# Low halves of the weights by an accumulating transfer: every fourth half unit of a split-fp32 decoder trunk

## The chip, the cores and the metric

The kernel runs on one core of a Trainium2 chip. The core has TensorE (in the profile PE for its matmuls and PEld for its weight loads), VectorE (DVE), ScalarE (ACT), GpSimd (POOL) and SyncE (SP, which here only issues transfers), 16 DMA engines, and its on-chip memories SBUF and PSUM. Each engine has a queue of its own and they wait for one another through semaphores. The metric is the time of one execution on the device in microseconds (us); lower is better.

## What is computed

The reference is a decoder trunk of two layers over 256 tokens of width 1024, in float32. Each layer is a half-step SwiGLU FFN, a mixer in which an SSD branch and a gated DeltaNet branch run side by side, and a second FFN:

```python
for l in range(DEPTH):
    h = h + 0.5 * swiglu(rms_norm(h, ffn1_norm[l]), ffn1_w_in[l], ffn1_w_out[l])
    u = rms_norm(h, mix_norm[l])
    (z_s, xbc, dt_s, qkv, z_d, b_d, a_d, gate_s, gate_d) = jnp.split(u @ w_in[l], split_points, axis=-1)
    y_s = mamba2_branch(...)
    y_d = deltanet_branch(...)
    merged = (jax.nn.sigmoid(gate_s) * (y_s @ ssm_w_branch[l])
              + jax.nn.sigmoid(gate_d) * (y_d @ dn_w_branch[l]))
    h = h + merged @ w_out[l]
    h = h + 0.5 * swiglu(rms_norm(h, ffn2_norm[l]), ffn2_w_in[l], ffn2_w_out[l])
return rms_norm(h, final_norm)
```

Nearly all of the work is matrix products with weights that are read once from HBM: 504 pieces of 128 x 1024 float32, 512 KB each.

## The kernel before

Precision comes from splitting. A float32 operand is written as a high part in the format float32r (fp32r in the profile) and a low part, the rest that the high part leaves; a product is then three matmuls: high by high, high by low, low by high. The activations are split when they are produced (uTh and uTl for the normed input, gh and gl inside the FFN, bh and bl in the branches, mh and ml for the merged output). The weights are split when they arrive.

The weights lie in the one array `wst`, in the order in which they are used. A *half unit* j is half of one of its rows, a tile of 128 x 1024. Three functions handle them:

- `load(j)` (line 93) issues the transfer of half j on SP into a buffer `wraw`, of which there are NRAW = 5.
- `prep(j)` (line 98) takes the raw tile, gets buffers `whi` and `wlo` (NSPL = 5 of each), lets ACT copy the raw tile into `whi` in float32r (line 102, shown as L60 in the profile because the helper `act` records it), and lets DVE subtract: `wlo` = `wraw` - `whi` (line 103, shown as L63, the helper `tt`).
- `take()` (line 111) hands the next half to the matmuls. It first issues the loads up to 9 halves ahead, and the preps up to 5 halves ahead. With five buffers the prep of half j can begin when the matmuls on half j-5 are done.

At the end of an FFN and of a mixer (`close`) the last five halves are taken together, and `state["hold"]` keeps further preps back until the norm that follows has its own instructions in the queues; `norm_in` then lets them go in small steps.

The users of the halves are: `tok_chunk` (four halves at a time, or two; tiles f and t), `chan_chunk` (two halves, 48 matmuls with 256 moving columns each; tiles fc in the FFN, kk, qq, vv, bc, zd, xs and g in the mixer), `branch` (two halves; b) and `out_chunks` (one, two or five halves; o). One FFN takes 66 halves: 4, then 40 in twenty chan chunks, then 22. A mixer takes 120. A layer is 252 halves, a multiple of four. In a chan chunk the order is: two passes, each over the eight row blocks, first the four of the first half, then the four of the second. The weights of the chan chunks and branches are the stationary operand; in the others they are the moving one.

The list ORDER sets by hand in which sequence the mixer's chunks and its small steps follow one another. The order of instructions on each engine is otherwise the scheduler's, by priority and by order in the program; the norms run with raised priority (`tc.high_priority(offset=PRI)`).

POOL has little to do: the inverse square roots as a power (`rsqrt`, line 118, in the profile L119; tiles zz, so, srr and c) and some memsets.

Of the kernel before, what the change touches and what calls it, by code (L numbers as in the profile page):

```python
# [11 lines left out]
ALU = mybir.AluOpType  # L12
# [33 lines left out]
def trunk_kernel(ctx, tc, x, wst, wsm, norms, lpar, rpar, cst, out):  # L46
    nc = tc.nc
    V, A, G, PE = nc.vector, nc.scalar, nc.gpsimd, nc.tensor
# [10 lines left out]
    def act(o, i, func=AF.Copy, **kw):  # L59
        return A.activation(out=o, in_=i, func=func, **kw)  # L60

    def tt(o, a, b, op):
        return V.tensor_tensor(out=o, in0=a, in1=b, op=op)  # L63
# [9 lines left out]
    def f(ap):  # L73
        return ap.bitcast(F32)
# [23 lines left out]
    def prep(j):  # L98
        r = raws.pop(j)
        hi = wpool.tile([P, 1024], F32R, tag="whi", name="whi", bufs=NSPL)  # L100
        lo = wpool.tile([P, 1024], F32R, tag="wlo", name="wlo", bufs=NSPL)
        act(hi[:], r[:])
        tt(lo[:], r[:], f(hi[:]), ALU.subtract)
        halves[j] = (hi, lo)

    def ahead(key, n, fn):
# [4 lines left out]
    def take():  # L111
        j = state["taken"]
        state["taken"] = j + 1
        ahead("loaded", j + NSPL + NRAW - 1, load)
        ahead("prepped", j + 1 if state["hold"] else j + NSPL, prep)
        return halves.pop(j)
# [46 lines left out]
    def rstd_of(t):  # L163

        ss = small([P, 2], "ss")
        for n in range(2):
            junk = tmp2("junk")
            act(junk[:], h[:, t, n * 512 : (n + 1) * 512], AF.Square, scale=1.0 / 32.0, accum_out=ss[:, n : n + 1])
        z = small([P, 2], "zz")
        ts(z[:, 0:1], ss[:, 0:1], ss[:, 1:2], ALU.add, EPS, ALU.add)  # L170
        rsqrt(z[:, 1:2], z[:, 0:1], [P, 1])
        return z[:, 1:2]
# [18 lines left out]
    def norm_in(nw, add=None):  # L191

        for t in range(2):
            with tc.high_priority(offset=PRI):
                if add:
                    add(t)
                ins, done = rms_chain(t, nw)
            if t == 0:
                state["hold"] = False
                n = state["taken"]  # L200
                if not add:
                    ahead("prepped", n + 1, prep)
                    with tc.issue_after(done[0].ins), tc.issue_after(done[1].ins):
                        ahead("prepped", n + START, prep)
                with tc.issue_after(ins.ins):
                    ahead("prepped", n + 2, prep)
# [819 lines left out]
    for t in range(2):  # L1026
# [5 lines left out]
        r = rstd_of(t)  # L1032
# [123 lines left out]
```

## Time and profile before

| | |
|---|---|
| time before, median of 2 runs | 1603.12 us (1601.9 to 1604.35) |
| span of the profiled execution, first to last instruction | 1602.4 us |
| granted TensorE clock, mean | 0.999 |
| HBM read | 280.94 MB |
| bytes moved by transfers | 284.86 MB, mean 178 GB/s |
| DMA engines, share of their time in packets (main queue) | 53.2% |

The page gives a span for the profiled execution and no other time of it; the span differs from the median of the runs by 0.7 us. The page lists the busy time of each engine, the same in 40 slices, the transfers' queues, the chain of work that ended last and the costliest groups of instructions, each as "line, engine, operation, output <- inputs, shape, count | busy us, mean ns of one | idle time of the engine just before them and what ended it". A timeline row is "start, duration, engine, line, operation, output <- inputs, shape, count [idle before <- what ended it]". A row of a tile's view gives "minimum/median/maximum duration in ns, first to last start in us".

### The profile page before, as it was taken

What the parts mean: (1) busy time and instruction counts of PE and PEld (TensorE: products, weight loads), DVE (VectorE), ACT (ScalarE), POOL (GpSimd) and SP (SyncE); (2) the same over time, 40 slices, a digit from 0 to 9 for tenths busy, and PEclk for the clock granted to TensorE, in tenths of its full rate; (3) what the DMA queues carried; (4) which work ended last, traced back from release to release, by engine and by line L of the source; (5) the groups of instructions that cost most, each with busy time, mean ns of one, the idle gap of its engine ahead of it and who ended that gap; (6) DMA issues with size and microseconds to landing.
All of it is one profiled execution on the core that took longest, in us unless ns stands there. A gap on an engine that the chain in (4) does not pass through costs nothing.

```text
span 1602.4 us, 30733 instructions
## 1 busy us (share of the span) xinstructions
PE 1582.4 (99%) x12624; PEld 1470.5 (92%) x12624; DVE 1068.2 (67%) x1546; ACT 882.5 (55%) x1418; POOL 59.1 (4%) x60
## 2 busy tenths in 40 slices
PE   8999999999999999999999999999999999999998
PEld 7999879999999998999899987899999999989986
DVE  5555468957899667555465555699579986665554
ACT  5444468756665545444354444686656664454443
POOL 0000020000000000000000001000000000000000
PEclk9999999999999999999999999999999999999999
DMA  7555465553455446555565555555335554555552
GB/s 263 191 187 195 162 203 189 165 156 117 170 199 177 143 161 201 191 187 197 171 205 190 185 197 179 188 182 186 115 130 201 170 172 159 180 174 188 191 199 94
DMA packets 91923, 284.86 MB, mean 178 GB/s; under 512 B 22069, under 2 KB 23045, under 8 KB 90758
## 3 DMA queue, kind: packets, MB, share of 16 engines
q1 hardware_dynamic: 91782, 282.90, 53.2%
q8 instruction: 99, 1.62, 0.4%
q14 instruction: 42, 0.34, 0.1%
HBM read 280.94 MB, written 1.92 MB: 177 GB/s over the span
## 4 chain that ended last, share of the span: by engine, by line
PE 91%; DVE 4%; DMA 2%; ACT 1%; POOL 1%; issue 1%; SPq 0%; POOLq 0%; DVEq 0%; ACTq 0%
PE fc L215 9%; PE fc L216 9%; PE fc L217 9%; PE o L211 5%; PE o L210 5%; PE o L209 5%; PE b L216 3%; PE b L217 3%; PE b L215 3%; PE t L209 2%; PE t L210 2%; PE xs L216 2%; PE xs L215 2%; PE t L211 2%; PE xs L217 2%; PE g L217 1%
## 5 line engine op out<-in xcount | busy, mean ns | idle before, releaser
L63 DVE TENSOR_TENSOR wlo<-wraw,whi 128x1024 fp32r<-128x1024 f32 x504 | 612.4, 1223 | 382.1 <-ACT whi L60 379.8
L60 ACT ACTIVATE whi<-wraw 128x1024 fp32r<-128x1024 f32 x504 | 529.2, 1059 | 436.9 <-PE fc L216 177.2
L215 PE MATMUL fc<-uTh,whi 128*128 128x256 f32 x1280 | 357.9, 280 | 0.0
L216 PE MATMUL fc<-uTl,whi 128*128 128x256 f32 x1280 | 357.3, 279 | 0.0
L217 PE MATMUL fc<-uTh,wlo 128*128 128x256 f32 x1280 | 356.7, 279 | 0.0
L216 PEld LDWEIGHTS fc<-uTl,whi 128*128 128x128 f32 x1280 | 240.7, 188 | 0.2
L215 PEld LDWEIGHTS fc<-uTh,whi 128*128 128x128 f32 x1280 | 240.6, 188 | 0.2
L217 PEld LDWEIGHTS fc<-uTh,wlo 128*128 128x128 f32 x1280 | 240.6, 188 | 0.0
L209 PE MATMUL o<-whi,gh 128*128 128x512 f32 x352 | 137.3, 390 | 0.0
L210 PE MATMUL o<-wlo,gh 128*128 128x512 f32 x352 | 137.2, 390 | 0.0
L211 PE MATMUL o<-whi,gl 128*128 128x512 f32 x352 | 137.0, 389 | 0.0
L215 PE MATMUL b<-bh,whi 128*128 128x256 f32 x384 | 108.9, 286 | 1.2 <-ACT bh L60 1.2
L216 PE MATMUL b<-bl,whi 128*128 128x256 f32 x384 | 108.5, 283 | 0.7 <-DVE bl L63 0.7
L217 PE MATMUL b<-bh,wlo 128*128 128x256 f32 x384 | 108.1, 283 | 0.0
L211 PEld LDWEIGHTS o<-whi,gl 128*128 128x128 f32 x352 | 66.1, 188 | 13.6
L209 PEld LDWEIGHTS o<-whi,gh 128*128 128x128 f32 x352 | 66.1, 188 | 13.5
L210 PEld LDWEIGHTS o<-wlo,gh 128*128 128x128 f32 x352 | 66.1, 188 | 13.5
L215 PEld LDWEIGHTS b<-bh,whi 128*128 128x128 f32 x384 | 73.2, 192 | 1.7 <-ACT bh L60 1.7
L216 PEld LDWEIGHTS b<-bl,whi 128*128 128x128 f32 x384 | 73.6, 192 | 1.1 <-DVE bl L63 1.1
L217 PEld LDWEIGHTS b<-bh,wlo 128*128 128x128 f32 x384 | 73.5, 192 | 0.0
L215 PE MATMUL xs<-uTh,whi 128*128 128x256 f32 x256 | 73.0, 285 | 0.0
L215 PE MATMUL g<-uTh,whi 128*128 128x256 f32 x256 | 72.6, 284 | 0.0
(265 smaller groups left out, 3250.6 us busy)
## 6 DMA issues: line engine op xcount, KB each, us to landing
wraw<-in_wst_dram SPq DMA_DIRECT2D x504, 512.0 KB, 4.0
dc<-rdram SPq DMA_DIRECT2D x8, 1024.0 KB, 7.0
nw<-in_norms_dram SPq DMA_DIRECT2D x6, 512.0 KB, 4.9
gb<-rdram SPq DMA_DIRECT2D x8, 256.0 KB, 5.9
h<-in_x_dram SPq DMA_DIRECT2D x4, 256.0 KB, 3.2
out_dram<-fo SPq DMA_DIRECT2D x4, 256.0 KB, 2.3
dq<-X SPq DMA_DIRECT2D x2, 256.0 KB, 4.3
cs<-in_cst_dram SPq DMA_DIRECT2D x1, 384.0 KB, 9.7
```

What stands on the lines that cost most here:

```text
L60: return A.activation(out=o, in_=i, func=func, **kw)
L63: return V.tensor_tensor(out=o, in0=a, in1=b, op=op)
L209: PE.matmul(ps, lh, rh, start=start, stop=False)
L210: PE.matmul(ps, lh, rl, start=False, stop=False)
L211: PE.matmul(ps, ll, rh, start=False, stop=stop)
L215: PE.matmul(ps, wh, mh, start=start, stop=False, skip_group_check=shared)
L216: PE.matmul(ps, wh, ml, start=False, stop=False, skip_group_check=shared)
L217: PE.matmul(ps, wl, mh, start=False, stop=stop, skip_group_check=shared)
```

## The change

In `prep`, every half unit with j % 4 == 3 gets its low part another way. ACT first writes the negated high part into `wlo` (a second activation with scale -1), and then a transfer issued from POOL reads the same half of the weights from HBM once more and adds it onto `wlo`: -high + weight. The other three quarters of the halves keep the subtraction on DVE. The raw tile of such a half is read by the first copy alone.

```diff
         hi = wpool.tile([P, 1024], F32R, tag="whi", name="whi", bufs=NSPL)
         lo = wpool.tile([P, 1024], F32R, tag="wlo", name="wlo", bufs=NSPL)
         act(hi[:], r[:])
-        tt(lo[:], r[:], f(hi[:]), ALU.subtract)
+        if j % 4 == 3:
+            act(lo[:], f(hi[:]), scale=-1.0)
+            G.dma_start(lo[:], wst[j // 2, :, (j % 2) * 1024 : (j % 2 + 1) * 1024], accum_op=ALU.add)
+        else:
+            tt(lo[:], r[:], f(hi[:]), ALU.subtract)
         halves[j] = (hi, lo)
```

Of the 504 halves 126 take the new path, 63 in each layer.

## What was predicted

> **What bounds the kernel now.** I read the page's busy line and its list of groups first, then the view of who waited for whom, then the timeline of one repeating stretch, and last the transfers.
>
> ```profile
> span 1602.4 us, 30733 instructions
> PE 1582.4 (99%) x12624; PEld 1470.5 (92%) x12624; DVE 1068.2 (67%) x1546; ACT 882.5 (55%) x1418; POOL 59.1 (4%) x60
> ...
> PEclk9999999999999999999999999999999999999999
> ...
> L63 DVE TENSOR_TENSOR wlo<-wraw,whi 128x1024 fp32r<-128x1024 f32 x504 | 612.4, 1223 | 382.1 <-ACT whi L60 379.8
> L60 ACT ACTIVATE whi<-wraw 128x1024 fp32r<-128x1024 f32 x504 | 529.2, 1059 | 436.9 <-PE fc L216 177.2
> ```
>
> TensorE (PE) is busy for 1582.4 of 1602.4 us at full granted clock; 20.0 us, 1.2%, is all that any relief of another engine can win back. VectorE (DVE) spends 612.4 us on the 504 subtractions, but it idles 382.1 us before them, waiting for ScalarE's copy. The view of the tile wlo tells whether anybody waits for the subtraction:
>
> ```profile
> L63 DVE TENSOR_TENSOR wlo<-wraw,whi x504: 1208/1225/1228, 9.3 to 1583.2; 128x1024 fp32r<-128x1024 f32 x168
> ...
>   PEld stb L854: 2.0, 2
>   PEld ydb L861: 1.5, 2
>   PEld f L210: 0.5, 1
>   PEld xs L217: 0.3, 1
> ```
>
> PE waited 4.3 us in all for it. So what the change takes away costs almost nothing today, and the whole question is how late the new path delivers a quarter of the low halves.
>
> **How late it may be.** One repeating stretch inside the FFN, ACT and PE rows:
>
> ```profile
> 682.08 1.06 ACT L60 ACTIVATE whi<-wraw 128x1024 fp32r<-128x1024 f32 x1 [0.83 <-PE fc L216]
> ...
> 693.28 1.06 ACT L60 ACTIVATE whi<-wraw 128x1024 fp32r<-128x1024 f32 x1 [0.83 <-PE fc L216]
> 694.73 1.06 ACT L60 ACTIVATE whi<-wraw 128x1024 fp32r<-128x1024 f32 x1 [0.39 <-PE fc L216]
> ...
> 694.37 1.23 DVE L63 TENSOR_TENSOR wlo<-wraw,whi 128x1024 fp32r<-128x1024 f32 x1 [1.20 <-ACT whi L60]
> ...
> 701.83 0.28 PE L217 MATMUL fc<-uTh,wlo 128*128 128x256 f32 x1
> ```
>
> Five pairs of buffers (NSPL) go round, so the copy of half j starts when PE has done with half j-5: ACT is released by "PE fc". Half 215 (215 = 3 mod 4) is copied from 693.28 to 694.34, and its low part is first read at 701.83. Its slack, from the end of the copy to the first read, is 7.49 us; the subtraction uses 1.26 of it. The work of PE between release and read is fixed, so a low half that comes L us after the copy's end stops PE for L minus the slack, and PE has no reserve to catch up with.
>
> I worked out the same difference for all 126 halves with j % 4 == 3, from the 504 copies and the 3,424 matmuls that read wlo, put in the order in which the code takes the halves:
>
> ```profile
> L60 ACT ACTIVATE whi<-wraw x504: 1038/1061/1118, 8.3 to 1582.2; 128x1024 fp32r<-128x1024 f32 x168
> ...
> L217 PE MATMUL fc<-uTh,wlo x1280: 277/278/290, 26.0 to 1535.6; 128*128 128x256 f32 x183
> ...
> L210 PE MATMUL o<-wlo,gh x352: 389/389/477, 139.5 to 1595.1; 128*128 128x512 f32 x176
> ```
>
> 7 halves have under 4 us, 23 have 4 to 7, 54 have 7 to 8 (38 of the 40 in the FFN's fc chunks lie between 7.44 and 7.89), 42 have over 8. Summing max(0, L - slack) gives the stall: 16 us at L = 4.4, 23 at 5, 37 at 6, 50 at 6.5, 64 at 7, 82 at 7.5, 122 at 8, 208 at 9, 303 at 10. It bends at 7.5, where the fc halves come in. Two more of the rows behind it, the tightest and a wide one:
>
> ```profile
> 1582.16 1.06 ACT L60 ACTIVATE whi<-wraw 128x1024 fp32r<-128x1024 f32 x1 [1.66 <-PE o L211]
> ...
> 1584.90 0.39 PE L210 MATMUL o<-wlo,gh 128*128 128x512 f32 x1
> ...
> 769.70 1.06 ACT L60 ACTIVATE whi<-wraw 128x1024 fp32r<-128x1024 f32 x1 [1.66 <-PE o L211]
> ...
> 780.61 0.39 PE L210 MATMUL o<-wlo,gh 128*128 128x512 f32 x1
> ```
>
> Half 503 has 1584.90 - 1583.22 = 1.68 us (it is the last of a group of five that PE takes together), half 243 has 9.85.
>
> **The change part by part.** *Removed:* 126 subtractions, 126 x 1.223 = 154 us of DVE, off the path but for about a quarter of those 4.3 us: -1 us.
>
> *Added on ACT:* 126 negated copies, of the same shape as the copy: 126 x 1.059 = 133 us, which takes ACT from 882.5 to about 1016 us, still far from the bound. What stands behind each on ACT comes up to 1.06 us later: the next whi (due 0.39 us after the first copy) and the silu; both have the slack shown above. Where ACT feeds PE at once, at the norms, I allow 2 us in all. What hides the rest is PE's own work; were ACT the bound, all 133 would count.
>
> *Added on the path of each such half:* L is the sum of three terms. The negated copy, 1.06. The issue on POOL, which the trace of before does not show for a transfer: below it SP's 0.33 per issue, above it POOL's longest small instruction, 2.99; I take 0.87, the mean of its smallest ones, because nothing is computed there. And the transfer itself, from issue to landing:
>
> ```profile
> wraw<-in_wst_dram SPq DMA_DIRECT2D x504, 512.0 KB, 4.0
> dc<-rdram SPq DMA_DIRECT2D x8, 1024.0 KB, 7.0
> ...
> L95 SPq DMA_DIRECT2D wraw<-in_wst_dram x504: 327/328/1310, 2.5 to 1570.9; - x168
> ...
> DMA to landing us min/median/max: 2.9/4.0/10.3
> ...
> L119 POOL TENSOR_TENSOR zz<-zz,mhalf 128x1 f32<-128x1 f32 x14 | 12.1, 866 | 892.3 <-DVE zz L71 892.3
> ...
> 426.54 2.99 POOL L119 TENSOR_TENSOR so<-so,mhalf 128x4 f32<-128x4 f32 x1 [20.33 <-DVE so L66]
> ```
>
> No accumulating transfer is in this trace. From below it is a plain load of the same 512 KB (2.9 at best, 4.0 in the middle); from above, the load's worst, 10.3. It moves 512 KB from HBM and must also read the 512 KB that it adds to, so it stands between the plain load, 4.0, and the 1024 KB transfer, 7.0: I take the middle, 5.5. With 0.06 for two hand-overs (0.03 each, 694.34 to 694.37) L = 1.06 + 0.87 + 5.5 + 0.06 = 7.5, and the stall is 82 us. The ends: 1.06 + 0.33 + 2.9 + 0.06 = 4.4 gives 16 us; 1.06 + 0.87 + 7.0 + 0.06 = 9.0 gives 208; the load's worst each time would give over 500, which a median does not do.
>
> [...]
>
> *Added on POOL's queue:* 126 issues ahead of 38 small powers for the norms and gates. A POOL instruction that waits for the negated copy holds up a power behind it. 14 powers of the norms are followed at once by DVE and PE; at half an issue each that is 14 x 0.44 = 6 us at most, and I take 4. In the other direction, four memsets stand in a row at each mixer's start:
>
> ```profile
> 205.09 1.81 POOL L455 MEMSET Q<- 128x2048 f32 x1
> ...
> 210.34 1.81 POOL L455 MEMSET TT<- 128x2048 f32 x1
> ```
>
> They hold POOL from 205.09 to 212.15, while ACT copies the halves of the mixer's first chunks; an issue behind them comes up to 7 us late, which at two mixers is 14 us at worst. Half 71's copy ends only after them (212.97), so I take nothing and leave it to the range.
>
> *Added on the DMA engines:*
>
> ```profile
> 1420.00:1540.00 120.00, 120.00 (x998) 118.62 (x997) 68.41 (x76) 58.51 (x77) 0.00 (x0) 1.00 0.57 190
> ...
> ACT whi L60 <- DMA wraw<-in_wst_dram: 3.8, 2, 2.8
> ```
>
> Four loads take 0.57 of the 16 engines (last but one column). The stretch of four halves is 693.28 - 682.08 = 11.20 us, so a load takes 1.6 us and 4.8 us are free. An accumulation worth two loads raises the share to 0.86; one worth three fills it. Loads run several halves ahead (ACT waited 3.8 us for them in the whole span), so up to there they hide their delay: nothing.
>
> Sum: 82 + 4 + 2 - 1 = 87 us. The profiled span of 1602.4 is 0.7 below the median of 1603.12, so the forecast is 1603 + 87 = 1690 us.
>
> **The rivals.** *The transfer is hidden (not slower).* If the accumulation lands as fast as a quick load, L stays below about 5.7, the stall at 32 us, the sum within 2%: about 1625 us at L = 5. For it: 2.9 us is seen for 512 KB on these engines. Against: 30 halves have under 7 us, so some stall remains, and the median load, unaccumulated, is at 4.0. It decides below 3.7 us from issue to landing beside the 0.87. [...]
>
> *The accumulation is much dearer.* Worth three loads or more, the engines fill up, and L reaches 9 to 10: 208 to 303 us, 1810 to 1905. For it: read, read and write of the same rows, an issue path that this trace has never shown, and the bend at 7.5, past which each microsecond costs about 85 us. Against: 4.8 us are free per stretch.
>
> *It becomes faster.* Only PE's 20.0 us of idle time can go, 1.2%; that is under 2% even if all went.
>
> **How the numbers follow.** Forecast (L from 6.3 to 8.2, 1650 to 1745 us): 0.45. Dearer: 0.27. Hidden, up to 1650: 0.26, of which 0.06 lies above 2%. Faster: 0.02, for what I do not see. 2% is 32 us, about what a measurement of this kernel can tell from no change. So slower 0.45 + 0.27 + 0.06 = 0.78, same 0.20, faster 0.02. The range runs from 1625 (L = 5) to 1830 (L = 9.2), which leaves about one in ten at either end.
>
> **What would show it.** PE's idle time rises from 20 us to about 100, and the weight loads and matmuls that read wlo wait for the transfer, in fc chunks only just; PE's busy time stays near 1582. The new rows on ACT are 126 of 1.06 us, DVE's count of subtractions is 378. The transfer's time to landing near 5.5 us and POOL's issue near 0.87 confirm the two terms; a landing under 4 or above 8 us overturns the size, and a DMA share near 1.0 the mechanism. No PE wait on the transfer at all would make the whole reading wrong.

## The result and the profile after

The changed kernel takes 1824.87 us in the median of two runs (1822.3 to 1827.44) against 1603.12 before: 1.138 times as long, 95% interval 1.134 to 1.143. The profiled execution has a span of 1820.5 us, 4.4 below its median; against the span before that is 218.1 us more, and the accounts below are made from span to span.

The head of the page of the changed kernel, with the groups that answer to those quoted before:

```profile
span 1820.5 us, 30906 instructions
...
PE 1659.9 (91%) x12624; PEld 1526.2 (84%) x12624; DVE 927.0 (51%) x1420; ACT 1001.3 (55%) x1544; POOL 163.7 (9%) x186
...
PEclk9999899999989989999999999999999898899999
...
q0 software_dynamic: 18144, 66.07, 21.3%
...
L63 DVE TENSOR_TENSOR wlo<-wraw,whi 128x1024 fp32r<-128x1024 f32 x378 | 460.1, 1223 | 379.6 <-ACT whi L60 374.7
...
L105 POOL DMA_DIRECT2D wlo<-in_wst_dram x126 | 110.6, 878 | 1378.8 <-ACT wlo L60 797.2
...
L60 ACT ACTIVATE wlo<-whi 128x1024 fp32r<-128x1024 f32 x126 | 133.2, 1057 | 3.0
...
wraw<-in_wst_dram SPq DMA_DIRECT2D x504, 512.0 KB, 4.8
wlo<-in_wst_dram POOLq DMA_DIRECT2D x126, 512.0 KB, 7.2
dc<-rdram SPq DMA_DIRECT2D x8, 1024.0 KB, 8.7
```

DVE and ACT changed as the diff says: 126 subtractions fewer, 126 copies more. PE tells where the time is, and in two parts. It stood idle for 1820.5 - 1659.9 = 160.6 us, against 20.0 before: +140.6. And the same 12,624 matmuls kept it busy for 1659.9 us instead of 1582.4: +77.5. The sum is the whole 218.1 us.

The view of who waited for whom, PE's rows alone (us in total, times, longest), names the cause of the first part:

```profile
PE b L221 <- DMA wlo<-in_wst_dram: 32.3, 8, 5.3
PE o L214 <- DMA wlo<-in_wst_dram: 26.0, 9, 4.9
PE fc L221 <- DMA wlo<-in_wst_dram: 23.6, 15, 4.0
PE f L214 <- DMA wlo<-in_wst_dram: 14.6, 4, 4.0
PE t L214 <- DMA wlo<-in_wst_dram: 12.4, 4, 4.4
...
PE b L220 <- DVE bl L63: 9.7, 2, 5.2
```

PE waits for the accumulating transfer. With the rows left out above, these waits add up to 128.1 us, where before there was none; the other 12.5 of the 140.6 us are mostly PE waiting for DVE and ACT in the mixer. The long waits are not in the regular fc chunks (1.6 us each in the mean) but at the starts and ends of stages and in the branches (2.9 to 4.0 in the mean), where the slack was small. (Line numbers have moved by four: L221 is L217 of before, L214 is L210.)

The second part shows in one stretch of an FFN's fc chunk, PE rows of the timeline, and then the busy time by stretch around it (columns: stretch, its length, busy us and count of PE, PEld, DVE, ACT, POOL, then granted clock, DMA share, GB/s):

```profile
722.52 0.28 PE L219 MATMUL fc<-uTh,whi 128*128 128x256 f32 x1
722.63 0.28 PE L220 MATMUL fc<-uTl,whi 128*128 128x256 f32 x1
726.15 0.58 PE L221 MATMUL fc<-uTh,wlo 128*128 128x256 f32 x1 [3.24 <-DMA wlo<-in_wst_dram]
726.53 0.41 PE L219 MATMUL fc<-uTh,whi 128*128 128x256 f32 x1
...
725.97:729.38 3.41, 3.23 (x15) 3.23 (x16) 0.00 (x0) 0.00 (x0) 0.00 (x0) 0.50 0.87 320
729.40:733.00 3.60, 3.60 (x33) 3.60 (x33) 0.18 (x1) 2.61 (x4) 0.19 (x1) 1.00 0.24 81
```

Behind this pause of 3.24 us the granted clock falls to 0.50 for 3.41 us, and in that time PE gets through 15 matmuls where the next 3.60 us have 33. There are 34 such pieces before the last matmul, 23 of 3.41 us and 11 of 6.83, 153.6 us in all. PE is busy for 134.1 us of them (the rest is waiting); at half speed half of that, an estimated 67 us, is the price of the clock. Some 9 of the other 10 us are a matter of counting: a matmul's row is 0.28 us long while the next one starts 0.11 us after it (722.52 and 722.63), so the last matmul before each pause adds some 0.16 us to the busy time, and there are 58 more breaks in PE's work than before. These 9 us belong to the pauses.

### The profile page after: what moved, and what is told of

Its sections match the earlier page's. It is cut to its first block, busy times and chain, and to the rows that moved or that the text cites. A ratio compares the mean times of both kernels' runs of the same rounds, so it can differ in the third digit from the quotient of the medians.

```text
span 1820.5 us, 30906 instructions
## 1 busy us (share of the span) xinstructions
PE 1659.9 (91%) x12624; PEld 1526.2 (84%) x12624; DVE 927.0 (51%) x1420; ACT 1001.3 (55%) x1544; POOL 163.7 (9%) x186
## 3 DMA queue, kind: packets, MB, share of 16 engines
q0 software_dynamic: 18144, 66.07, 21.3%
## 5 line engine op out<-in xcount | busy, mean ns | idle before, releaser
L63 DVE TENSOR_TENSOR wlo<-wraw,whi 128x1024 fp32r<-128x1024 f32 x378 | 460.1, 1223 | 379.6 <-ACT whi L60 374.7
L221 PE MATMUL fc<-uTh,wlo 128*128 128x256 f32 x1280 | 362.9, 284 | 23.8 <-DMA wlo<-in_wst_dram 23.6
L221 PEld LDWEIGHTS fc<-uTh,wlo 128*128 128x128 f32 x1280 | 243.4, 190 | 28.2 <-DMA wlo<-in_wst_dram 27.6
L105 POOL DMA_DIRECT2D wlo<-in_wst_dram x126 | 110.6, 878 | 1378.8 <-ACT wlo L60 797.2
L214 PE MATMUL o<-wlo,gh 128*128 128x512 f32 x352 | 140.7, 400 | 10.5 <-DMA wlo<-in_wst_dram 10.4
L221 PE MATMUL b<-bh,wlo 128*128 128x256 f32 x384 | 117.6, 310 | 32.3 <-DMA wlo<-in_wst_dram 32.3
L60 ACT ACTIVATE wlo<-whi 128x1024 fp32r<-128x1024 f32 x126 | 133.2, 1057 | 3.0
L220 PE MATMUL b<-bl,whi 128*128 128x256 f32 x384 | 116.7, 305 | 9.7 <-DVE bl L63 9.7
L63 DVE TENSOR_TENSOR g<-sg,fc 128x256 f32<-128x256 f32 x80 | 33.4, 418 | 170.2 <-ACT sg L60 170.2
L221 PEld LDWEIGHTS b<-bh,wlo 128*128 128x128 f32 x384 | 82.7, 217 | 34.0 <-DMA wlo<-in_wst_dram 34.0
L220 PEld LDWEIGHTS b<-bl,whi 128*128 128x128 f32 x384 | 82.4, 215 | 10.1 <-DVE bl L63 10.1
L214 PEld LDWEIGHTS o<-wlo,gh 128*128 128x128 f32 x352 | 67.5, 192 | 27.6 <-DMA wlo<-in_wst_dram 13.7
L219 PEld LDWEIGHTS b<-bh,whi 128*128 128x128 f32 x384 | 81.7, 214 | 0.9 <-ACT bh L60 0.9
L221 PE MATMUL xs<-uTh,wlo 128*128 128x256 f32 x256 | 75.2, 294 | 6.0 <-DMA wlo<-in_wst_dram 5.9
```

Source lines behind the costliest of these rows:

```text
L105: G.dma_start(lo[:], wst[j // 2, :, (j % 2) * 1024 : (j % 2 + 1) * 1024], accum_op=ALU.add)
L214: PE.matmul(ps, lh, rl, start=False, stop=False)
L219: PE.matmul(ps, wh, mh, start=start, stop=False, skip_group_check=shared)
L220: PE.matmul(ps, wh, ml, start=False, stop=False, skip_group_check=shared)
L221: PE.matmul(ps, wl, mh, start=False, stop=stop, skip_group_check=shared)
```

## The experiments

One explanation had to be kept apart from its rivals. Theory A: the low half lands after PE wants it, and a longer pause of PE also costs clock behind it. Against it stood that ACT's extra copies cost (B), that every transfer costs the same through traffic or its queue (C), that the way through POOL is slow and not the add (A2), and that the transfers, not the pauses, lower the clock (D).

Each run is compared with runs of the kernel before made beside it; their medians are 1603.46 to 1603.62 us (1603.12 for the changed kernel).

| run | what stands in prep for the chosen halves | us | PE idle | PE busy over before | clock |
|---|---|---|---|---|---|
| before | subtraction | 1603.1 | 20.0 | 0 | 0.999 |
| changed | accumulating transfer, 126 halves | 1824.9 | 160.6 | 77.5 | 0.957 |
| e1 | negated copy, then an addition on DVE, 126 | 1611.0 | 21.3 | 2.8 | 0.998 |
| e2 | plain transfer, 126 | 1689.9 | 81.1 | 26.5 | 0.986 |
| e3 | clears and subtraction on POOL, 126 | 1703.8 | 86.4 | 33.2 | 0.991 |
| e4 | accumulating transfer, 90 with much slack | 1679.0 | 64.7 | 23.3 | 0.988 |
| e5 | accumulating transfer, 36 with little slack | 1767.7 | 129.3 | 57.1 | 0.962 |
| e6 | as the change, six split buffers | 1694.7 | 82.6 | 32.5 | 0.983 |
| e7 | as before, six split buffers | 1624.3 | 34.6 | 6.9 | 0.996 |
| e8 | clears and subtraction on POOL, the same 36 | 1738.4 | 108.8 | 48.0 | 0.971 |
| e9 | accumulating transfer, 32 with the most slack | 1623.8 | 32.7 | 7.0 | 0.993 |
| e10 | accumulating transfer, 40 fc halves | 1640.4 | 49.1 | 13.0 | 0.994 |
| e11 | eight clears and subtraction on POOL, 40 fc halves | 1728.2 | 110.9 | 33.9 | 0.984 |
| e12 | ten clears and subtraction on POOL, 40 fc halves | 1704.8 | 85.5 | 36.0 | 0.983 |

PE idle is the span less PE's busy time; this, the busy time and the clock are those of the profiled execution. The busy time over before is not all the clock's: half of PE's busy time at half clock is 67 us in the changed kernel, 56 in e5 and 41 in e8, but only 13 of the 33 in e3, 14 of the 23 in e4 and 25 of the 34 in e11. The rest is in part the counting at pauses described above; it was not taken apart further.

### e1: the negated copy without the transfer

```diff
         if j % 4 == 3:
             act(lo[:], f(hi[:]), scale=-1.0)
-            G.dma_start(lo[:], wst[...], accum_op=ALU.add)
+            tt(lo[:], r[:], f(lo[:]), ALU.add)
```

> Theory A (the low half lands too late, and each longer pause of PE also costs clock): the negated copy stays, the transfer goes, so the low half is there about 2.4 us after the copy of the high half (1.06 + 1.22 + hand-overs); only the 4 halves with under 2 us of slack are late, each under 1 us. Time 1603 to 1612 us, PE idle under 30 us, granted clock 0.99 or more. Rival B (the 126 extra copies on ScalarE hold up its queue): at least 30 us of the loss stays, 1635 us or more.

1610.96 us, 1.0053 of before (1.0034 to 1.0071). PE idle is 21.3 us, 1.3 more than before. B falls: of the 222 us the copies on ACT, and the low half that comes a little later by them, hold about 8 (at most 11 by the interval).

### e4 and e5: the halves divided by their slack

The 126 halves were split by the slack that the trace of before gives them. In e4 the 36 tightest are subtracted as before; in e5 only these use the transfer (TIGHT is the list of the 36).

```diff
-        if j % 4 == 3:
+        if j % 4 == 3 and j not in TIGHT:      # e4
+        if j in TIGHT:                          # e5
```

> Only the 90 of the 126 halves that had 7.3 us of slack or more keep the accumulating transfer. Theory A: from the measured times to landing and the slack before, their stalls add up to 41 us, each too short for a drop of the clock: 1640 to 1660 us, clock 0.99 or more. Rival C (each transfer costs the same, by traffic or by its queue: 218 / 126 = 1.73 us): 90 x 1.73 = 156 us, 1759 us, clock about 0.97.

> Only the 36 halves with under 7.3 us of slack keep the accumulating transfer. Theory A: about 100 us of stall and nearly all of the 78 us of slower matmuls come from them: 1750 to 1790 us, clock 0.96 to 0.97. Rival C: 36 x 1.73 = 62 us, 1665 us, clock about 0.99.

e5 has 29% of the transfers and 164 us, three quarters of the loss: 1767.71 us, ratio 1.1013 (1.096 to 1.1066), inside theory A's range and 100 us from C's. e4 has 71% of the transfers and 75 us: 1679.0, ratio 1.0462 (1.0435 to 1.0489); that is 80 us from C, but 19 above A's upper end, and the clock of 0.988 is below A's 0.99: seven pauses were followed by half clock. In the waits of e4 some 20 us more than before are none of the transfer's:

```profile
PE fc L224 <- DMA wlo<-in_wst_dram: 17.1, 19, 3.5
PE b L223 <- DVE bl L66: 9.7, 2, 5.5
PE stb L861 <- DVE xe L66: 7.1, 2, 4.0
PE xsb L850 <- ACT xsT L63: 5.4, 2, 3.6
...
DVE dc L66 <- DMA dc<-rdram: 24.4, 6, 6.3
```

In the mixer DVE waits 24.4 us for the 1024 KB load of dc (2.3 before), and PE waits for DVE and ACT there. C is wrong as the main cause. That the added traffic makes these waits is not shown: in e7, which adds no transfer, dc lands after 9.4 us in the median and DVE waits 2.6 us; in e2 it lands after 7.0, as before, and DVE waits 12.7. What the traces do show is another order on DVE. In the first layer of the changed kernel a dc load is issued at 478.23 and DVE is ready to read it at 483.75, with one subtraction in between; before, the same load is issued at 443.29 and read at 454.61, with three. DVE comes to the load earlier and so waits for it. What part of PE's 20 us this is was not separated.

### e2: the same transfer without the add

```diff
-            G.dma_start(lo[:], wst[...], accum_op=ALU.add)
+            G.dma_start(lo[:], wst[...])
```

> The transfer from GpSimd stays, behind the same negated copy, but overwrites the low buffer with the weights and does not add (the low part is then the weight itself). Theory A1 (the second read for the add makes it late): time to landing falls from 7.2 to about 5.2 us (issue 0.88 plus a plain load's 4.0 to 4.8), the low half is there after 6.6 us, the stalls fall to about 55 us and the drops of the clock with them: 1660 to 1700 us. Rival A2 (it is the way through GpSimd, not the add): landing stays near 7 us, time near 1825 us.

1689.89 us, within the range of A1. The transfers' rows of e2, and POOL's issue:

```profile
q0 software_dynamic: 18144, 66.07, 12.5%
...
wraw<-in_wst_dram SPq DMA_DIRECT2D x504, 512.0 KB, 4.4
wlo<-in_wst_dram POOLq DMA_DIRECT2D x126, 512.0 KB, 5.0
...
L105 POOL DMA_DIRECT2D wlo<-in_wst_dram x126 | 68.4, 543 | 1302.9 <-ACT wlo L60 743.9
```

With the same queue, packets and bytes, the plain transfer lands after 5.0 us, the accumulating one after 7.2. These times include POOL's issue, which is 0.54 us for the plain and 0.88 for the accumulating transfer. In engine time the plain one takes 0.125 x 1690.0 / 126 = 1.68 us, the accumulating one 0.213 x 1820.5 / 126 = 3.08: 1.84 times as much. So the add makes it late by 2.2 us, 0.3 of them in the issue, and the way through POOL (5.0 against SP's 4.4, with 0.54 and 0.33 of issue in them) adds little. That a second read makes it late, as A1 has it, is not shown: both runs list the same 18,144 packets and 66.07 MB.

### e6 and e7: one more pair of split buffers

```diff
-NRAW = 5
-NSPL = 5
+NRAW = 3
+NSPL = 6
+NGRP = 5     # the groups in close keep their five
```

> The changed kernel with six pairs of split buffers and three raw buffers in place of five and five; the groups at the stage ends stay at five. Each half may then be copied one half unit earlier, about 2.8 us more slack. Theory A: with a mean delay of 8.9 us and 2.8 us more slack the stalls fall from 141 to about 30 us and the clock's loss from 78 to under 20: 1630 to 1670 us. Rival B2 (the cost lies in traffic or queues, not in lateness): still above 1780 us.

> The kernel before with the same six and three buffers: what the buffers do by themselves. Nothing waits for a low half there, so 1598 to 1612 us by each theory.

With the landing unchanged (7.3 us in the median) e6 takes 1694.65 us, ratio 1.0555 (1.0527 to 1.0582): 130 of the 222 us are gone with the same transfers in it, which B2 excludes; PE's waits for them in the fc chunks fall from 23.6 to 0.6 us. It is 25 us above A's range. e7 shows that the buffers themselves cost 21 us, 1624.29 (1.0128, 1.0112 to 1.0143), where I had expected no difference. Two raw buffers had to go for the sixth pair, and ACT waits 101.0 us for loads in e7 and 218.7 in e6, against 3.8 before; so in e6 many copies start later than the sixth pair would let them, and the added slack is less than the 2.8 us that A took. How these waits reach PE was not followed. Over e7 the transfers cost 70 us.

### e3 and e8: the same lateness without a transfer

```diff
-            act(lo[:], f(hi[:]), scale=-1.0)
-            G.dma_start(lo[:], wst[...], accum_op=ALU.add)
+            for _ in range(6):                  # e8: eight, and only for j in TIGHT
+                G.memset(f(lo[:]), 0.0)
+            G.tensor_tensor(out=lo[:], in0=r[:], in1=f(hi[:]), op=ALU.subtract)
```

> No added transfer: for the same 126 halves GpSimd clears the low buffer six times (about 0.9 us each by the 1.81 us for 128 x 2048) and then subtracts, so the low half is late by work on GpSimd alone. Theory A: where PE pauses for 1.75 us or more the clock drops to half behind it, so with pauses of that length the mean clock falls under 0.99 although not a byte more is moved. Rival D (the transfers' traffic or its power lowers the clock): clock 0.99 or more whatever PE waits.

> As the run with the 36 tight halves, but no transfer is added: for these halves GpSimd clears the low buffer eight times (0.96 us each) and subtracts (2.47 us), so that it is there some 9 us after the copy. Theory A: like the transfers on the same halves: PE idle 100 to 150 us, clock 0.955 to 0.975, 1740 to 1800 us, without a byte more. Rival D (the transfers lower the clock): clock 0.99 or more and PE busy under 1605 us.

e3 has a single run and does not decide: 86.4 us of idle time, most in pauses under 2 us, and a mean clock of 0.991, which by the bound that I had set speaks for D. Yet of its 13 pauses of 1.75 us or more, six were followed by half clock. e8 settles it: 1738.43 us (1.0842, 1.0819 to 1.0864; 2 us below the range), clock 0.971, PE busy 48.0 us longer, with 284.88 MB moved, as before (284.86). D falls: no byte is added, and the matmuls slow down all the same.

### e9 and e10: only where there is room

```diff
-        if j % 4 == 3:
+        if j in WIDE:                                                          # e9: the 32 with 9.7 us and more
+        if j % 4 == 3 and (4 <= j % 252 < 44 or 190 <= j % 252 < 230):         # e10: the fc chunks
```

> Only the 32 halves with 9.7 us of slack or more keep the accumulating transfer. Theory A: by the measured delays their stalls add up to 1.4 us; what remains is the mixer's 1024 KB load for dc, for which VectorE waits longer when more is moved (22.7 us against 2.3 in the changed kernel): 1605 to 1622 us, clock 0.995 or more. Rival C (1.73 us a transfer): 1659 us.

> Only the 40 halves of the FFN's fc chunks keep the accumulating transfer; 36 of them have 7.4 to 7.9 us of slack. Theory A: the stalls add up to 26 us in short pieces, the clock stays at 0.995 or more: 1625 to 1645 us, with PE busy under 1595 us. Rival C: 40 x 1.73 = 69 us, 1672 us, and the clock falls with it to about 0.985.

e10: 1640.4 us, ratio 1.0221 (1.0173 to 1.0269), in A's range in time and 32 us from C's figure. PE's busy time is 0.4 us above its bound (1595.4), and the clock of 0.994 is 0.001 below its own, since four of the pauses reach 2.5 to 4.4 us. PE waits 27.9 us for the transfer in 21 pieces, where the slacks and the landings gave 26.

e9: 1623.8 us, ratio 1.0124 (1.0109 to 1.0139), 2 us above A's range, 35 below C's. PE's waits of e9 hold 1.5 us for the transfer, where A had 1.4; what is left is the mixer again:

```profile
PE xsb L850 <- ACT xsT L63: 7.7, 2, 4.4
PE hnT L191 <- DVE hn L69: 5.4, 7, 1.6
PE stb L861 <- DVE xe L66: 3.2, 2, 1.8
...
DVE dc L66 <- DMA dc<-rdram: 16.3, 6, 4.0
...
PE qq L224 <- DMA wlo<-in_wst_dram: 0.8, 2, 0.4
```

So even a transfer that is hidden almost altogether gains nothing, and 32 of them cost 20 us: 12.7 us more of PE's idle time, and 7.0 more of busy time behind three pauses that were followed by half clock. Which of the mixer's waits come from the transfers, and which from an order of the instructions that the scheduler made otherwise, was not separated.

### e11 and e12: regular pauses of two lengths

The block of e3 with eight (e11) and ten (e12) clears, for the 40 fc halves of e10.

> No added transfer: for the 40 halves of the fc chunks GpSimd clears the low buffer eight times and subtracts: 8 x 0.96 + 2.47 = 10.15 us after the buffers come free, against 8.6 us until PE reads. Theory A: regular pauses of about 1.65 us, 40 x 1.65 = 66 us, below the 1.75 us from which pauses were followed by a drop: clock 0.99 or more, PE busy under 1600 us, 1660 to 1680 us.

> The same with ten clears: 12.07 us, pauses of about 3.6 us. Theory A: 40 x 3.6 = 144 us of pauses, and behind each at least one stretch of 3.41 us at half clock, 40 x 1.7 = 68 us of slower matmuls that move not a byte more: 1790 to 1840 us, clock about 0.93, PE busy 1640 to 1660 us. Rival D (pauses cost only themselves; the clock follows the transfers): 1750 us, clock 0.99 or more.

Both left their ranges, in time and in clock, because the pauses did not have the lengths that were planned. e11's average 91.3 / 40 = 2.3 us, not 1.65: the subtraction takes 2.73 us there in the mean, not 2.47. In e12 the order of ACT's copies changed with the length of POOL's work, and its pauses average 64.1 / 40 = 1.6 us, the longest 2.2, so that it is faster than e11. As a pair on the two sides of 1.75 us they fail. Nor is a drop behind every pause: of the 34 pauses of 1.75 us or more in e11 only 15 were followed by half clock (15 times 3.41 us is 51; the mean clock of 0.984 over 1727.2 us stands for about 55 us at 0.50, the end of the span included). Each run still shows the drop without any added transfer, as in this stretch of e11 (columns as above):

```profile
74.57 0.27 PE L221 MATMUL fc<-uTl,whi 128*128 128x256 f32 x1
77.75 0.58 PE L222 MATMUL fc<-uTh,wlo 128*128 128x256 f32 x1 [2.91 <-POOL wlo L106]
...
74.85:77.62 2.77, 0.00 (x0) 0.00 (x0) 0.98 (x2) 0.00 (x0) 2.77 (x1) 1.00 0.60 189
77.64:81.05 3.41, 3.29 (x15) 3.30 (x16) 0.00 (x0) 0.00 (x0) 0.06 (x1) 0.50 0.70 253
81.10:84.50 3.40, 3.40 (x31) 3.40 (x30) 0.00 (x0) 2.09 (x3) 2.23 (x3) 1.00 0.14 55
```

POOL alone is late here, and the picture is that of the changed kernel: a pause, 3.41 us at 0.50 with 15 matmuls, then 31 in the same time.

## Why the prediction was right and wrong

*The direction and the first half of the mechanism: right.* Removing the subtractions gained nothing, the low halves came after PE wanted them, and the size of the loss is set by the slack of each half. e1, e5, e6 and e9 show it from four sides.

*The step that failed:* "PE's busy time stays near 1582". The sum priced a pause at its own length. In the changed kernel each of the 34 pauses of 1.75 us or more is followed by at least 3.41 us at half clock. That cost 67 us on top, 2 us a pause: half of the 131 us by which the sum of 87 fell short of 218.1. The trace of before could not show it as a price: from the first matmul on its longest pause of PE is 1.2 us, and its clock falls only behind the last matmul.

*The term that was mis-sized:* L. The view of the tile wlo in the changed kernel:

```profile
DMA to landing us min/median/max: 5.3/7.2/12.0
```

That includes POOL's issue, 0.878 us against the 0.87 taken. That this fits is luck: the 0.87 came from small powers, and a plain transfer's issue took 0.54 in e2. The transfer is then 6.3 in the median and not 5.5. The hand-over from ACT to POOL took 0.29 us in most cases, not 0.03, and in the mixer the negated copy itself stood up to 5 us behind others on ACT. Averaged over the 126 halves L was 8.9 us, not 7.5. PE idle grew by 140.6 us where 82 were forecast: 58.6 us of the miss. Taking the middle of two distant rows was the weak choice: beside the issue, a plain transfer from POOL already took 4.5 us in e2, not 4.0, and the add put 1.8 on top.

*The stall curve.* With each half's own L and its slack before, the sum of max(0, L - slack) is 191 us, not 140.6. Nine halves at the starts and ends of stages hold 55 of these without their cost: there, by the order of before, the low half would be read before it had landed, so PE must have read others first. Less these, 136 us stand against the 128.1 that PE waited for the transfer and the 140.6 of all idle time added.

*The small terms.* 4 us for POOL's queue and 2 for ACT cannot be told apart in the result; e1's 8 us are a bound for the second that is above it. DMA engines: with 0.72 to 0.81 of their time in the FFNs they did not fill, as forecast, but the loads' landing rose from 4.0 to 4.8 and that of dc from 7.0 to 8.7. "Nothing" was wrong at dc: DVE waited 22.7 us for it instead of 2.3. As e2 and e7 show, the landing alone does not make this wait, and its cause stays open.

*The rivals.* "Hidden" needed a landing of 3.7 us beside the issue; even the plain transfer of e2 has 5.0 - 0.54 = 4.5. "Much dearer" named the right time, 1810 to 1905, by the wrong way. Its L of 9 nearly came (8.9), but neither by three loads' worth (in engine time it is 1.84 plain ones) nor by full engines, and its 208 us of stall did not come: PE stood still for 140.6 us more, and the clock behind the pauses did most of the rest (67 of 77.5 us). For the same reason it is luck that 1824.87 us lies inside the range, 1625 to 1830: its upper end stood for stall alone.

## What to carry to other kernels

Where PE is the bound, work taken off another engine is worth only the time PE waits for that engine (4.3 us here); price the new path by its delay against the slack of every single use, and put it where the slack is widest, not at every fourth place. (Here no place gained anything: the 32 widest still cost 20 us.) A pause of PE can cost more than its length: in the changed kernel half clock stood behind all 34 pauses of 1.75 us or more and added an estimated 2 us a pause, though in e11 it stood behind only 15 of 34. The accumulating transfer of 512 KB took 3.08 us of engine time against 1.68 for a plain one of the same size, 1.84 times as much, and landed 2.2 us after it (7.2 against 5.0).

## What the runs showed of the hardware

In the trace of the changed kernel the starts of the stretches at half clock lie whole multiples of 3.413 us apart, to within 0.003 us, and the stretches last 3.41 us (23 of them) or 6.83 (11). The time of this execution can be cut into windows on that grid, and only windows at full clock, up to the last matmul, be taken. Every window behind which the clock fell to 0.50 had at least 1.75 us in which PE stood still; no window behind which it stayed had more than 1.89. Between the two figures both happened, so the idle time of a window does not decide alone. What else does was not shown.

Nor does the length of a pause decide alone: in the changed kernel all 34 pauses of 1.75 us or more were followed by half clock, in e11 15 of 34. That a pause's place on the grid counts beside its length is my reading of this, which no run was made to show; by it a part of the 67 us is where the pauses happened to fall.
